# The embedding's rows split early, kept in HBM and fetched by transposing transfers

## The chip, the cores and the metric

The kernel runs on one core of a Trainium2 chip. The time is the device time of one execution in microseconds. Lower is better.

## What is computed

One layer of a hybrid decoder over 2048 prompt tokens and 32 sample tokens (8 sequences of 4), model width 1024: a gated linear attention branch and a causal convolution branch side by side, merged, projected and added to x; then a gate with an embedding that is an input of its own for every token (256 wide). The change touches the last lines of it:

```python
x = x + merged @ w_o
x = x + jax.nn.sigmoid(x @ w_pg) * (p @ w_pe)      # p: (tokens, 256), w_pe: (256, 1024)
y = rmsnorm(x, g_final)
```

## The kernel before, in words

Matrix products are made in f16 with split operands: each f32 operand becomes a high half and a low half (`hl`, L669: one ScalarE operation for the high half, one VectorE operation for the low half), and a product is three matmuls (high by high, high by low, low by high). TensorE contracts over the partitions, so an activation has to stand with its channels on the partitions before it can be an operand.

The last stage (from L664, in the tile pool `p4`) works on pairs of token tiles, 2 x 128 tokens, eight pairs, in two passes:

- The first pass (loop at L846) loads x for the pair from the input, multiplies the merged branches by w_o in a seven-product scheme (`split_forms`, `halves`, L691 to L711, 84 matmuls of 512 columns a pair), adds the results to x in place (`Residual`, L777) and stores x in `x1_d` in HBM (L851). After the first pair the 14 forms of w_pg are loaded and split, two steps a pair.
- The second pass (loop at L866) loads x from `x1_d` (L868), transposes it on TensorE (`transposed`, L839), makes its forms and multiplies them by w_pg in the same scheme. `Gate` (L791) takes each quarter of the result as it comes: `gate` (L750) makes `p @ w_pe` for it (three matmuls for each of two chunks of the embedding, L274 to L276), then tanh, product and sum, and `finish` (L761) makes the norm and stores y.

The embedding comes in through `load_p` (L738): the tile `pr` (128 tokens x 256, f32) is loaded over SP's queue, TensorE transposes it in two pieces (L746) into a PSUM tile, and `hl` (L747) writes the halves `pT`. `Gate.__init__` calls it twice a pair; the 32 sample rows get one call of their own. `pr`, `pT` and the f16 forms have 2, 2 and 10 buffers; x has 4, two pairs' worth.

Loads go over SP's queue (`dma`), stores and accumulating loads over POOL's (`store`). The order on each engine and queue is set by a planner ahead of time from program order and estimated times, and the engines then run in that order: an instruction that waits holds up all behind it on its engine.

Of the kernel before, what the change touches and what calls it, by code (L numbers as in the profile page):

```python
# [9 lines left out]
F32 = mybir.dt.float32  # L10
F16 = mybir.dt.float16
# [8 lines left out]
P = 128  # L20
D = 1024
T = 2048
# [12 lines left out]
PLE = 256  # L35
# [6 lines left out]
SX = 2.0 ** 3  # L42
# [44 lines left out]
def hybrid_step(ctx: ExitStack, tc, A, O):  # L87
    nc = tc.nc
# [8 lines left out]
    dram = ctx.enter_context(tc.tile_pool(name="dram", bufs=1, space=bass.MemoryType.DRAM))  # L97
# [6 lines left out]
    def dma(out, in_):  # L104
        return nc.sync.dma_start(out=out, in_=in_)

    def store(out, in_):
        return nc.gpsimd.dma_start(out=out, in_=in_)
# [7 lines left out]
    def sm_tile():  # L116
        return smp.tile([P, 512], F32, tag="sm", name="sm")
# [101 lines left out]
    def load_w(src, c0, width=P, k0=0, nk=KC, pool=None):  # L219

        c0 = [c0] if isinstance(c0, int) else c0
        w = (pool or wpool).tile([P, 2, nk, len(c0) * width], F16, tag="w", name="w")
        st = wst.tile([P, nk, len(c0) * width], F32, tag="st", name="st")
        for i, c in enumerate(c0):
            wdma(st[:, :, i * width:(i + 1) * width], src[k0 * P:(k0 + nk) * P, c:c + width].rearrange("(k p) c -> p k c", p=P))
        split_w(w[:, 0], w[:, 1], st)
        return w
# [104 lines left out]
    with sb_pool("pg", 2) as pg, sb_pool("p0", 2) as p0:  # L332
# [16 lines left out]
        for gi, nt in enumerate(P0_GROUPS):  # L349
# [9 lines left out]
            r = xt[0][1]  # L359
# [257 lines left out]
    for blk, (a, n, aT, bT, _) in enumerate(ops):  # L617
# [4 lines left out]
        for c in range(KC):  # L622
            m = []
            for i, (w, act, d) in enumerate(((wA[c], aT, ta_d), (wB[c], bT, tb_d))):
                t = p3.tile([P, DB], F32, tag=f"t{i}", name=f"t{i}", bufs=T_BUFS[i])[:, 0:n]
# [27 lines left out]


    x1_d = dram.tile([P, TT // P + 1, D], F32, name="x1_d")
    pp = A["p_prompt"][0, 0]
    psm = A["p_sample"][0].rearrange("b t d -> (b t) d")
    yp = O["y_prompt"][0]
# [5 lines left out]
    with sb_pool("p4", 2) as p4:  # L664
# [4 lines left out]
        def hl(dst, src, sc):  # L669
            S.activation(dst[:, 0], src, AF.Copy, scale=sc)  # L670
            V.scalar_tensor_tensor(out=dst[:, 1], in0=src, scalar=sc, in1=dst[:, 0], op0=MULT, op1=SUB)

        def split_forms(t, sc):

            a11, a12, a21, a22 = (t[:, 4 * k:4 * k + 4, i * P:(i + 1) * P] for i in range(2) for k in range(2))
            sums = [p4.tile([P, 4, P], F32, tag="sum", name="sum", bufs=3) for i in range(3)]
            F = {f: p4.tile([P, 2, 4, P], F16, tag="f", name="f", bufs=10) for f in (A11, A12, S2, S1, S3, A22, S4)}
            hl(F[A11], a11, sc)
            hl(F[A12], a12, sc)
            V.tensor_tensor(out=sums[0], in0=a21, in1=a22, op=SUB)  # L680
            V.tensor_tensor(out=sums[1], in0=sums[0], in1=a11, op=SUB)
            hl(F[S2], sums[1], sc)
            hl(F[S1], sums[0], sc)
            V.tensor_tensor(out=sums[2], in0=a11, in1=a21, op=SUB)
            hl(F[S3], sums[2], sc)
            V.tensor_tensor(out=sums[1], in0=a12, in1=sums[1], op=ADD)
            hl(F[S4], sums[1], sc)
            hl(F[A22], a22, sc)
            return F

        def halves(F, W, got, cut=False):  # L691

            def prod(ps, fa, fb, start, cols=((0, 512),)):
                for c0, w in cols:
                    for k in range(4):
                        for p in range(3):
                            PE.matmul(ps[:, c0:c0 + w], lhsT=F[fa][:, p == 2, k], rhs=W[fb][k // 2][:, p == 1, k % 2, c0:c0 + w],  # L697
                                      start=start and k + p == 0, stop=k == 3 and p == 2, skip_group_check=not start)
            X, Z, Y = mm_tile(), fl_tile(), fl_tile()
            prod(X, A11, B11, True)  # L700
            r1 = got.keep(X, 1)
            prod(Z, A12, B21, True)
            got(0, 0, r1, 1, Z)
            prod(X, S2, T2, False)
            r2 = got.keep(X, 2)
            prod(Y, S1, T1, True)
            y1 = got.part22(Y)
            prod(X, S3, T3, False)
            prod(Y, S4, B22, False)
            got.rest22(y1, X)  # L710
            got(0, 1, r2, -1, Y)  # L711
            prod(X, A22, T4, False, ((0, 256), (256, 256)) if cut else ((0, 512),))
            got(1, 0, None, 0, X)
# [8 lines left out]
        def dec_parts(t, sc):  # L722
            dT = p4.tile([P, 2, 12, TD], F16, tag="dT", name="dT", bufs=1)
            hl(dT[:, :, 0:4], t[:, 0:4], sc)
            hl(dT[:, :, 4:8], t[:, 0:4], -sc)
            hl(dT[:, :, 8:12], t[:, 4:8], sc)
            return dT

        def dec_rows(j, dT, W):
            ps = mm_tile()  # L730
            rows_halves(ps, j, dT, W)
            t = p4.tile([P, 512], F32, tag="tg", name="part", bufs=2)
            S.copy(t, ps)
            ps = fl_tile()
            PE.matmul(ps[0:TD], lhsT=sel[:, 0:TD], rhs=t, start=True, stop=True)
            return ps[0:TD]

        def load_p(i, r):  # L738

            pr = p4.tile([P, PLE], F32, tag="pr", name="pr")  # L740
            dma(pr[0:r], pp[i * P:i * P + r] if i < 16 else psm)
            pT = p4.tile([P, 2, 2, P], F16, tag="pT", name="pT")
            pt = sm_tile()
            pv = pt.rearrange("p (k t) -> p k t", t=P)[:, 0:2, 0:r]
            for k in range(2):
                PE.transpose(pv[:, k], pr[0:r, k * P:(k + 1) * P], ident[0:r, 0:r])  # L746
            hl(pT[:, :, :, 0:r], pv, SX)  # L747
            return pT
# [42 lines left out]
        class Gate:  # L791
            def __init__(self, x, a, last):
                self.x, self.last, self.a = x, last, a
                self.pT = [load_p(a // P + i, P) for i in range(2)]
                self.ss = [p4.tile([P, 4], F32, tag=f"ss{i}", name="ss") for i in range(2)]
                self.n = [0, 0]
# [26 lines left out]
        def x_tile(src, r=P):  # L823
            if r == P:
                x = [p4.tile([P, D], F32, tag="x", name="x", bufs=4) for _ in range(2)]
            else:
                x = [p4.tile([r, D], F32, tag="xd", name="xd", bufs=1)]
            for i, t in enumerate(x):
                dma(t, src(i))
            return x  # L830
# [15 lines left out]
        for pair in range(npair):  # L846
            a = pair * 2 * P
            x = x_tile(lambda i: xf[a + i * P:a + (i + 1) * P])
            halves(split_forms(mT[pair], sc), w_o, Residual(x))
            for i in range(2):  # L850
                store(x1_d[:, 2 * pair + i], x[i])  # L851
            if pair == dec_at:
                x = x_tile(lambda i: xs, TD)
                dT = dec_parts(mT[npair], sc)
                res = Residual(x)
                for j in range(2):
                    res.add(0, j, 1, dec_rows(j, dT, w_o))
                store(x1_d[0:TD, 2 * npair], x[0])
            if pair == 0:
                w_pe = [load_w(A["w_pe"][0], 0, D, k, 1, pool=pool) for k, pool in enumerate((wpool, wpool2))]  # L860
                halves8 = (t[:, i] for _ in range(7) for t in [mpool.tile([P, 2, 2, 2, 512], F16, tag="m", name="wf")] for i in range(2))
                steps = load_forms(A["w_pg"][0], halves8, True)
                w_pg = next(steps)
            for _ in range(2):
                next(steps, None)
        for pair in range(npair):  # L866
            last = pair == npair - 1
            x = x_tile(lambda i: x1_d[:, 2 * pair + i])  # L868
            halves(split_forms(transposed(x, P), SE), w_pg, Gate(x, pair * 2 * P, last), last)
            if pair == dec_at:  # L870
                x = x_tile(lambda i: x1_d[0:TD, 2 * npair], TD)
                pT = load_p(16, TD)
                dT = dec_parts(transposed(x, TD)[:, :, 0:TD], SE)
                ss = p4.tile([P, 4], F32, tag="ss0", name="ss")[0:TD]
                for j in range(2):
                    gate(x[0], ss, j, TD, pT, dec_rows(j, dT, w_pg), j * 512, 512)
                finish(x[0], ss, 2, TD, ysm)
# [265 lines left out]
```

## Time and profile before

| | |
|---|---|
| time, median of 3 runs | 2420.59 us (2420.32 to 2424.48) |
| the profiled execution | 2422.98 us |
| its span, first to last instruction | 2421.2 us |
| TensorE busy | 2326.5 us (96%) |
| VectorE, ScalarE, GpSimd busy | 1678.6, 858.5, 439.5 us |
| last stage, first pass | about 2040 to 2197 us |
| last stage, second pass | about 2197 to 2406 us, then 15 us of finishing |

The profile is one execution. "Busy" counts an engine's running instructions; matmuls overlap, so that a matmul's duration is longer than the time that it adds, and the time from start to start is the one to add up. PE is TensorE, PEld its weight loads, DVE VectorE, ACT ScalarE, POOL GpSimd, SP SyncE, which here only issues transfers. L746 is line 746 of the kernel.

### The profile page before, as it was taken

Reading aid. Unit: us, or ns where it says so; the run is one execution under the profiler, and the core shown is the slowest. Engines: PE = TensorE matmul, PEld = TensorE weight load, DVE = VectorE, ACT = ScalarE, POOL = GpSimd, SP = SyncE. Lnnn points to the kernel's source line nnn. Section 1 sums busy time; section 2 is a strip of 40 time slices with the busy share of each in tenths; the row PEclk is TensorE's granted clock in tenths of the full one; section 3 lists DMA queues with packets and bytes.
Section 4 is the critical chain, followed back from the end, with each engine's and each line's share of the span. In section 5 each row is a group of like instructions: output and inputs, shape, how many; then the busy total and the mean of one; then the engine's idle time right before and its main releaser. Section 6 shows DMA issues by size and latency. Waiting matters only on the chain.

```text
span 2421.2 us, 43469 instructions
## 1 busy us (share of the span) xinstructions
PE 2326.5 (96%) x16909; PEld 1462.8 (60%) x16909; DVE 1678.6 (69%) x3835; ACT 858.5 (35%) x2043; POOL 439.5 (18%) x965
## 2 busy tenths in 40 slices
PE   5899999999999999999999989999999999999997
PEld 3445555655556655555655556556999997444544
DVE  6666996595784875783973965645577788865666
ACT  6552123223223224223233224444233434323544
POOL 1011212221222122222131222121000000111333
PEclk8999999999999999999999999999999999999999
DMA  7322202103221113220123220236345536743222
GB/s 221 111 95 71 59 19 72 34 28 112 66 58 31 35 51 96 62 69 22 31 69 93 55 82 30 82 98 186 100 116 131 130 100 183 202 125 102 90 81 74
DMA packets 193350, 210.04 MB, mean 87 GB/s; under 512 B 39419, under 2 KB 164665, under 8 KB 191608
## 3 DMA queue, kind: packets, MB, share of 16 engines
q1 hardware_dynamic: 169032, 132.28, 20.8%
q0 software_dynamic: 24112, 74.99, 8.9%
q8 instruction: 132, 2.16, 0.4%
q14 instruction: 74, 0.61, 0.1%
HBM read 138.33 MB, written 69.72 MB: 86 GB/s over the span
## 4 chain that ended last, share of the span: by engine, by line
PE 76%; DMA 7%; DVE 6%; issue 4%; POOL 4%; ACT 2%; SPq 0%; DVEq 0%; POOLq 0%; ACTq 0%
PE mm L274 13%; PE mm L275 13%; PE mm L276 13%; PE fl L274 7%; PE fl L275 7%; PE fl L276 7%; PE mm L697 5%; PE fl L697 4%; DMA stf<-in_w_in 2%; POOL ms L196 1%; PE sm L1048 1%; DVE acc L516 1%; PE sm L1049 1%; PE sm L1050 1%; DMA st<-in_w_pg 1%
## 5 line engine op out<-in xcount | busy, mean ns | idle before, releaser
L274 PE MATMUL mm<-xT,w 128*128 128x416 f16 (+2 forms) x1216 | 363.2, 304 | 3.3 <-DVE zz L947 1.7
L275 PE MATMUL mm<-xT,w 128*128 128x416 f16 (+2 forms) x1216 | 363.4, 304 | 0.0
L276 PE MATMUL mm<-xT,w 128*128 128x416 f16 (+2 forms) x1216 | 362.9, 304 | 0.0
L274 PE MATMUL fl<-xT,wf 128*128 128x416 f16 x960 | 329.7, 344 | 12.5 <-DVE ob L327 11.8
L275 PE MATMUL fl<-xT,wf 128*128 128x416 f16 x960 | 329.5, 343 | 0.0
L276 PE MATMUL fl<-xT,wf 128*128 128x416 f16 x960 | 329.1, 343 | 0.0
L516 DVE SCALAR_TENSOR_TENSOR acc<-ue,kvec,acc 128x1024 f32<-128x1024 f32 (+1 forms) x232 | 290.0, 1272 | 0.0
L275 PEld LDWEIGHTS <-w 128*128 128x128 f16 x2496 | 243.2, 98 | 68.3 <-issue 10.3
L274 PEld LDWEIGHTS <-w 128*128 128x128 f16 x2496 | 243.2, 98 | 59.4 <-issue 2.3
L276 PEld LDWEIGHTS <-w 128*128 128x128 f16 x2496 | 243.2, 98 | 57.3 <-issue 2.2
L697 PEld LDWEIGHTS <-f 128*128 128x128 f16 x1356 | 132.5, 98 | 159.4 <-issue 6.2
L275 PE MATMUL mm<-w,xT 128*128 128x512 f16 x512 | 195.1, 381 | 0.0
L276 PE MATMUL mm<-w,xT 128*128 128x512 f16 x512 | 195.1, 381 | 0.0
L274 PE MATMUL mm<-w,xT 128*128 128x512 f16 x512 | 194.9, 381 | 0.0
L697 PE MATMUL mm<-wf,f 128*128 128x512 f16 (+1 forms) x780 | 180.6, 379 | 5.8 <-ACT f L670 3.7
L274 PE MATMUL fl<-bT,w 128*128 128x208 f16 x640 | 161.7, 253 | 0.6 <-ACT ob L325 0.6
L274 PE MATMUL mm<-aT,w 128*128 128x208 f16 x640 | 161.3, 253 | 0.5 <-DMA aT<-a_d 0.5
L275 PE MATMUL fl<-bT,w 128*128 128x208 f16 x640 | 161.7, 253 | 0.0
L276 PE MATMUL fl<-bT,w 128*128 128x208 f16 x640 | 161.7, 253 | 0.0
L276 PE MATMUL mm<-aT,w 128*128 128x208 f16 x640 | 161.5, 253 | 0.0
L275 PE MATMUL mm<-aT,w 128*128 128x208 f16 x640 | 161.5, 253 | 0.0
L516 DVE SCALAR_TENSOR_TENSOR acc<-acc,ksum 128x1024 f32<-128x1024 f32 x120 | 152.5, 1270 | 0.0
(281 smaller groups left out, 4030.8 us busy)
## 6 DMA issues: line engine op xcount, KB each, us to landing
x<-in_x_prompt SPq DMA_DIRECT2D x32, 512.0 KB, 8.0
st<-in_w_in SPq DMA_DIRECT2D x24, 512.0 KB, 10.2
stf<-in_w_in SPq DMA_DIRECT2D x42, 256.0 KB, 6.7
zz_d<-ob POOLq DMA_DIRECT2D x40, 208.0 KB, 2.4
ta_d<-ob POOLq DMA_DIRECT2D x40, 208.0 KB, 2.3
tb_d<-ob POOLq DMA_DIRECT2D x40, 208.0 KB, 2.6
cv<-cv_d SPq DMA_DIRECT2D x80, 104.0 KB, 2.0
zz<-zz_d SPq DMA_DIRECT2D x80, 104.0 KB, 2.1
```

What stands on the lines that cost most here:

```text
L196: E.tensor_scalar(out=x, in0=x, scalar1=scale, scalar2=EPS, op0=MULT, op1=ADD)
L274: PE.matmul(out, lhsT=lh, rhs=rh, start=(k == 0), stop=False)
L275: PE.matmul(out, lhsT=lh, rhs=rl, start=False, stop=False)
L276: PE.matmul(out, lhsT=ll, rhs=rh, start=False, stop=(k == nk - 1))
L516: V.scalar_tensor_tensor(out=out[:, 0:n], in0=src[:, j:j + n], scalar=w1[:, j:j + 1], in1=out[:, 0:n], op0=MULT, op1=ADD)
L697: PE.matmul(ps[:, c0:c0 + w], lhsT=F[fa][:, p == 2, k], rhs=W[fb][k // 2][:, p == 1, k % 2, c0:c0 + w], start=start and k + p == 0, stop=k ...
L1048: PE.matmul(po[:, c], lhsT=qe[:, cc], rhs=st_prev, start=True, stop=False)
L1049: PE.matmul(po[:, c], lhsT=att[:, c], rhs=v[:, c], start=first, stop=True)
L1050: PE.matmul(pu[:, c * DV:(c + 1) * DV], lhsT=kdT[:, cc], rhs=v[:, c], start=True, stop=True)
```

## The change

`split_p`, new, is called in the first pass for each of the pair's two token tiles, right behind the store of x: it loads the tile's embedding rows, splits them as they are (tokens on the partitions) and stores both halves in a new HBM tensor `p_d` of f16. `load_p` no longer loads, transposes and splits for prompt tiles: it issues two transposing transfers on SP's queue, one for each half, that bring the 128 x 256 block of `p_d` into `pT` with the channels on the partitions. For the sample rows all stays as it was. `ph`, the tile that `split_p` fills, takes its two buffers from the same tag as `pT`.

```diff
+    p_d = dram.tile([T, 2, PLE], F16, name="p_d")
...
+        def split_p(i):
+
+            pr = p4.tile([P, PLE], F32, tag="pr", name="pr")
+            dma(pr, pp[i * P:(i + 1) * P])
+            ph = p4.tile([P, 2, 2, P], F16, tag="pT", name="ph").rearrange("p h k t -> p h (k t)")
+            hl(ph, pr, SX)
+            store(p_d[i * P:(i + 1) * P], ph)
+
         def load_p(i, r):
 
+            pT = p4.tile([P, 2, 2, P], F16, tag="pT", name="pT", bufs=2)
+            if r == P:
+                for h in range(2):
+                    nc.sync.dma_start_transpose(out=pT[:, h], in_=p_d[i * P:(i + 1) * P, h])
+                return pT
             pr = p4.tile([P, PLE], F32, tag="pr", name="pr")
-            dma(pr[0:r], pp[i * P:i * P + r] if i < 16 else psm)
-            pT = p4.tile([P, 2, 2, P], F16, tag="pT", name="pT")
+            dma(pr[0:r], psm)
...
             for i in range(2):
                 store(x1_d[:, 2 * pair + i], x[i])
+                split_p(2 * pair + i)
```

## Rows read from the trace of the kernel before

**Rows 1.** The page: busy time and share; TensorE's granted clock in 40 slices

```profile
PE 2326.5 (96%) x16909; PEld 1462.8 (60%) x16909; DVE 1678.6 (69%) x3835; ACT 858.5 (35%) x2043; POOL 439.5 (18%) x965
...
PEclk8999999999999999999999999999999999999999
```

**Rows 2.** Busy time by stretches: the two passes, then three pairs

```profile
core 0: us, PE busy (x) PEld busy (x) DVE busy (x) ACT busy (x) POOL busy (x), PEclk, DMA share, GB/s
2040.00:2196.80 156.80, 154.63 (x750) 68.81 (x749) 110.50 (x167) 50.11 (x76) 18.65 (x24) 0.98 0.58 172
2196.80:2406.30 209.50, 209.50 (x1092) 104.14 (x1091) 136.77 (x224) 102.69 (x225) 70.12 (x136) 1.00 0.25 83
2225.15:2250.64 25.49, 25.49 (x130) 12.87 (x129) 17.34 (x29) 12.70 (x28) 9.99 (x19) 1.00 0.28 93
2250.64:2276.14 25.50, 25.50 (x131) 12.90 (x129) 17.30 (x29) 12.70 (x28) 9.97 (x19) 1.00 0.28 93
```

**Rows 3.** The chain that ended last, over one pair: start, us, what

```profile
2225.15 0.44 PE sm L746 x4
2225.59 2.59 PE fl L697 x12
...
2238.32 0.22 PE sm L276
2238.54 2.59 PE mm L697 x12
2241.13 2.59 PE fl L697 x12
2243.72 0.44 PE sm L839 x4
...
2250.64 0.44 PE sm L746 x4
2251.08 2.59 PE fl L697 x12
2253.67 0.22 PE sm L274
```

**Rows 4.** Groups by shape, 2196 us to the end: busy us, mean ns

```profile
L671 DVE SCALAR_TENSOR_TENSOR pT<-sm,pT 128x256 f16<-128x256 f32 x16 | 6.3, 410 | 0.0
L670 ACT ACTIVATE pT<-sm 128x256 f16<-128x256 f32 x16 | 5.6, 386 | 0.4 <-PE sm L746 0.4
...
L746 PE MATMUL sm<-ident,pr 128*128 128x128 f32 x32 | 5.3, 273 | 0.0
```

**Rows 5.** Busy time by stretches of 20 us, first pass, columns as in rows 2

```profile
2040.00:2060.00 20.00, 18.69 (x77) 7.80 (x76) 17.74 (x31) 8.06 (x14) 1.26 (x1) 0.87 0.79 249
2060.00:2080.00 20.00, 19.83 (x93) 8.91 (x92) 17.75 (x28) 8.72 (x14) 3.59 (x4) 1.00 0.73 190
2080.00:2100.00 20.00, 20.00 (x94) 9.11 (x93) 16.36 (x25) 7.53 (x12) 2.33 (x3) 1.00 0.67 193
2100.00:2120.00 20.00, 20.00 (x95) 9.05 (x93) 16.64 (x25) 6.66 (x10) 4.16 (x5) 1.00 0.81 227
```

**Rows 6.** Waits in the first pass: us in total, times, longest us

```profile
DVE wf L237 <- ACT wf L236: 10.9, 7, 3.1
...
PE mm L697 <- DVE x L777: 1.2, 3, 0.7
```

**Rows 7.** Waits of SP's queue in the first pass, same columns

```profile
SPq L105 <- DMA x_d<-x: 118.0, 15, 16.1
```

**Rows 8.** Instructions on the tensor x_d: duration in ns, min/median/max

```profile
L108 POOL DMA_DIRECT2D x_d<-x x16: 531/558/1045, 2067.1 to 2198.0; - x16
```

**Rows 9.** Timeline of SP's queue: start, us, transfers issued

```profile
2040.56 3.02 SPq L105 DMA_DIRECT2D x<-in_x_prompt  x4
...
2044.27 1.81 SPq L105 DMA_DIRECT2D pr<-in_p_prompt  x2
...
2225.40 0.80 SPq L105 DMA_DIRECT2D pr<-in_p_prompt  x2
2237.08 2.03 SPq L105 DMA_DIRECT2D x<-x_d  x2
```

**Rows 10.** Issue to landing: the tile pr; x loads at 2237 us (last column)

```profile
DMA to landing us min/median/max: 1.9/2.1/11.8
...
x<-x_d SPq DMA_DIRECT2D x2, 512.0 KB, 4.1
```

**Rows 11.** Timeline of TensorE ahead of the first pass: idle time before it, releaser

```profile
2038.73 1.03 PE L697 MATMUL mm<-wf,f 128*128 128x512 f16 x2 [3.67 <-ACT f L670]
```

## The prediction

> **What bounds the kernel now.** I read the page first: TensorE is busy 96% of the span, no other engine over 69%, and its granted clock is over 0.9 of full speed (2.4 GHz) from the second slice on [rows 1]. A busy share is an average, so next the table by stretches, cut at the two passes of the last stage [rows 2]. The second pass (2196.8 to 2406.3 us) has TensorE busy for all of its 209.50 us at full clock, and one pair of token tiles recurs every 25.49 us with 25.49 us of TensorE. In the first pass (2040.0 to 2196.8) TensorE has 154.63 of 156.80 us, and most of the missing 2.2 us lies in the first 20 us. So in both passes the end moves only if TensorE gets less to do, or if something makes it wait. Next the chain of waits over one pair [rows 3]: it stays on TensorE without a break, so its pieces are the issue slots, and their sum is the period. Last the groups by shape, the 20 us stretches of the first pass, the waits and SyncE's queue (SP), for what would be late if something slipped [rows 4 to 11].
>
> **What is removed.** The 32 f32 transposes of the embedding leave the second pass, four a pair. The chain gives them 0.44 us per four [rows 3]; eight pairs make 8 x 0.44 = 3.5 us. It is the slot that counts, not the 273 ns duration of one [rows 4], since durations overlap: 84 products and 24 embedding matmuls at 0.216 us (12 take 2.59), 16 transposes of x and 4 of the embedding at 0.109 us sum to 18.14 + 5.18 + 1.74 + 0.44 = 25.5 us, the period. Since TensorE has no idle time there, the whole 3.5 us comes off, and what is late next is TensorE still: a pair should take 25.05 us. The two transposes of the sample rows stay. Sixteen pairs of a split's two operations (ScalarE 386 ns, VectorE 410 ns each [rows 4]) leave the pass as well; both engines have over 8 us of room in each period [rows 2], so that is worth nothing.
>
> **What is moved to the first pass.** The splits: 16 x 0.386 = 6.2 us of ScalarE and 16 x 0.410 = 6.6 us of VectorE, the price with a PSUM source, taken for the SBUF source too. On average there is room: VectorE is busy 110.5 of 156.8 us, ScalarE 50.1 [rows 2]. But in the first 40 us VectorE is busy 17.7 of 20 us [rows 5], and its update of x (L777) must read a PSUM bank before TensorE may accumulate into it again. The engines run in order, so a split that waits for its rows holds up that update, the other splits and the forms behind it. The trace prices such a wait: VectorE stood 10.9 us, in 7 waits, for the high half of a w_pg form, and TensorE waited for x only 1.2 us in 3 [rows 6], so about 0.11 us for each us lost on VectorE. With 6.6 us of work and about as much waiting the loss is 13 x 0.11 = 1.4 us. Bounds: 0 if all of it falls into VectorE's gaps; 10 us if each of the 6.6 us of work delays a PSUM read directly and the first pair of loads is waited for as well. I take 1 us, nearer to the row, since that was measured with the same kind of wait.
>
> **The transfers of the first pass.** Sixteen loads of 128 KB move to it and sixteen stores of 128 KB are new (128 rows x 512 f16), 4.2 MB. The pass moves 172 GB/s at a DMA share of 0.58 [rows 2], so 297 GB/s when full, and 4.2 MB are 14 us of full DMA: share 0.67 if spread out, 0.93 if all of it falls in the first 80 us, where the share is 0.67 to 0.81 [rows 5]. Two embedding loads already stood there, queued behind four x tiles, and took 11.8 us to land [rows 9, 10]. On SP the loads come between x loads that wait up to 16.1 us for an earlier store of x [rows 7], and the split behind waits with them. On POOL the stores cost 16 x 0.56 = 9 us of issue at the price of a store of x [rows 8], on an engine that is busy 18.65 of 156.8 us; behind a store that waits for its split stand the stores of x (which free buffers for x loads) and the accumulating w_pg loads. All of this is inside the 0 to 10 us above.
>
> **What is added to the second pass.** Thirty-two transposing transfers of 64 KB on SP, four a pair. No such transfer is in this trace. They need a free pT buffer, which the pair before releases with its last embedding matmul (2238.54), and are wanted at 2253.67 [rows 3], so 15.1 us cover four of them. The nearest rows are the plain 128 KB loads of the same rows: 0.40 us to issue and 2.1 us to land in the median, 11.8 us at worst [rows 9, 10]. With four at 0.40 us and 2.1 us they are there by 2242.3; even at 11.8 us for the last it is 2251.9. I take nothing. The upper end is open: if each of the four ran alone and took more than 3.8 us, TensorE would wait.
>
> The traced row has TensorE's transpose at a 0.109 us slot. The Trainium skill's page "VectorE: DVE Perf Modes", in the rules for kernel authors, speaks against this change: transpose 128x128 on TensorE if PSUM will do as the target, and through the DMA crossbar otherwise. Its section on the three transpose paths gives 1309 ns for a crossbar transpose of 128x128; by that, eight such tiles a pair in a row would be an estimated 10.5 us. That is under the 15.1 us, so the sum would be the same by the page; no run here shows it yet.
>
> **The sum.** The profiled execution took 2422.98 us around a span of 2421.2. It becomes 2422.98 - 3.5 + 1.0 = 2420.5. That execution is 2.4 us above the median of the timed ones, 2420.59, so I lower the median by the same 2.5 us: 2418. Only a difference over 0.2%, 4.8 us, can be told from no change by timing this kernel; the forecast is inside that.
>
> **Rivals.**
> 1. *The transposing transfers stand ahead of the x loads on SP.* Two x loads per pair are released by a store, here at 2237.08 [rows 9], and the pT buffers at 2238.54 by TensorE: the planner's order on SP hangs on 1.5 us. If the four transfers come first, x goes 1.5 us later plus four issues of 0.40 to 1.0 us [rows 9], so at 2240.1 to 2242.5; with 4.1 us to land [rows 10] it is there at 2244.2 to 2246.6, wanted at 2243.72 [rows 3]. TensorE then waits 0.5 to 2.9 us in each of the six pairs whose x is loaded like that: 3 to 17 us, say 1.3 x 6 = 8 us. Time: 2418 + 8 = 2426, slower than before. It decides from 4.8 + 2.5 = 7.3 us of waiting, 1.2 us a pair. For it: the 2.5 us in which x is ready ahead of use are thin. Against it: x comes earlier in the program and is released first.
> 2. *The splits hurt the first pass.* Loads late in a stretch with full DMA queues, ScalarE and VectorE waiting in order. Priced at 8 us, in the upper half of its bounds: 2420.6 - 3.5 + 8 = 2425. For it: the 11.8 us and VectorE's 17.7 of 20 us. Against it: DVE's 10.9 us of waits cost TensorE almost nothing.
> 3. *A transpose costs TensorE its duration.* 32 x 0.273 = 8.7 us off: 2420.6 - 8.7 = 2412. Against it: the slots of 0.109 us sum to the period. The Trainium skill's page "TensorE: Matmul & The Clock Gate", section on the PE-mode transpose, gives about 275 ns for one in a kernel, which is the duration of the row; taken as a price it would give this case.
> 4. *The change doesn't do what it says*: the transfers don't fit under the 15.1 us. With 5.2 us for each of four in a row, 20.8 us, TensorE waits 5.7 us in seven pairs: 2418 + 40 = 2458. Waits that long may also lower its clock: after 3.67 us of idle time ahead of the first pass [rows 11] the granted clock was 0.87 over its first 20 us [rows 5].
>
> **How the numbers follow.** Forecast 0.51 (own range 2414.5 to 2422.5), rival 1 0.14, rival 2 0.18, rival 3 0.10, rival 4 0.07. Faster by over 0.2% (under 2415.7): rival 3 and 0.04 of the forecast, 0.14. Slower (over 2425.4): 0.10 of rival 1, 0.09 of rival 2, rival 4, 0.01 of the forecast, 0.27. The rest, 0.59, is within 0.2%. The range takes in forecast, rival 2, half of rival 3 and most of rival 1: 2412 to 2431.
>
> **What would show it.** Right: pairs of the second pass at 25.05 us, TensorE still without idle time there, the first pass still near 156.8 us long. Rival 1 shows as TensorE waiting for x at L839, with SP's four transfers before the x loads; rival 2 as TensorE waiting for x at L777 or a form, behind a split that waits for its load; rival 3 as pairs of 24.4 us; rival 4 as TensorE waiting for pT at L274. The prediction is wrong if the pairs don't shorten by 0.44 us, or if either pass shows TensorE idle for over 5 us.

## The result, and the profile after

| | before | after |
|---|---|---|
| time, median | 2420.45 us (2418.84 to 2424.48) | 2439.23 us (2436.12 to 2443.12) |
| ratio, 95% interval | | 1.0084 [1.0069, 1.0098] |
| the profiled execution, its span | 2422.98, 2421.2 us | 2440.28, 2438.5 us |

The change makes the kernel 18.8 us slower. The prediction had 2418 us and a range up to 2431: wrong in sign and size.

From the page of after, what answers to [rows 1]: TensorE busy, and its granted clock in 40 slices.

```profile
PE 2326.3 (95%) x16877; PEld 1458.6 (60%) x16877; DVE 1681.1 (69%) x3835; ACT 860.9 (35%) x2043; POOL 447.9 (18%) x981
...
PEclk8999999999999999999999999999999999999999
```

These rows hardly show 18.8 us: the same busy time and clock digits, a span 17.3 us longer. (Further down, the page has 17.3 us of idle time ahead of the products at L698, 10.8 of it ended by an update of x, where before has 5.8.) So I cut the last stage at its products, which are the same in every kernel here: the first pass from the start of the first product with w_o to that of the first with w_pg, the second from there to the start of the last; a pair is 84 of them. Busy time of after by passes, which answers to the first two of [rows 2]:

```profile
core 0: us, PE busy (x) PEld busy (x) DVE busy (x) ACT busy (x) POOL busy (x), PEclk, DMA share, GB/s
2034.37:2206.08 171.71, 159.83 (x752) 70.15 (x753) 117.23 (x185) 55.98 (x95) 27.80 (x40) 0.95 0.63 183
2206.08:2425.50 219.42, 210.92 (x1082) 103.05 (x1079) 134.78 (x210) 100.91 (x212) 67.81 (x136) 0.99 0.25 79
```

Cut in the same way, before takes 158.40 and 211.51 us. The first pass is 13.3 us longer and the second 7.9. TensorE stands idle for 11.9 us of the first (2.2 in before) and for 8.5 us of the second (none in before). (The first product starts at 2034.4 in after and at 2038.7 in before; over the profiled kernels that start lies between 2032.2 and 2038.7. So I compare lengths of passes, not ends.)

**The first pass, pair by pair.** The first three pairs of before, then its seventh, columns as above:

```profile
2038.73:2061.43 22.70, 21.23 (x84) 8.67 (x85) 20.41 (x36) 10.35 (x20) 1.26 (x1) 0.86 0.78 243
2061.43:2079.56 18.13, 18.13 (x84) 8.22 (x84) 15.89 (x25) 6.85 (x11) 3.59 (x4) 1.00 0.76 197
2079.56:2097.69 18.13, 18.13 (x85) 8.23 (x84) 14.49 (x22) 7.23 (x12) 2.33 (x3) 1.00 0.65 186
2158.90:2177.02 18.12, 18.12 (x85) 8.22 (x84) 8.20 (x14) 3.15 (x5) 1.08 (x2) 1.00 0.32 117
```

The first three of after:

```profile
2034.37:2059.05 24.68, 21.41 (x85) 8.63 (x86) 21.36 (x39) 11.43 (x23) 2.78 (x3) 0.86 0.79 239
2059.05:2078.89 19.84, 18.29 (x84) 8.22 (x84) 16.31 (x28) 7.18 (x14) 5.64 (x8) 1.00 0.81 207
2078.89:2106.67 27.78, 21.22 (x85) 8.94 (x84) 19.64 (x32) 10.07 (x18) 6.88 (x12) 0.82 0.74 226
```

They lose 2.0, 1.7 and 9.7 us, the whole 13.3; each of the other five pairs is within 0.3 us of before. Though two splits a pair are written in the program, the planner had moved all 16 into the first 80 us (their stores go out from 2047.9 to 2112.2), where VectorE had least room; in the seventh pair it works 8.20 of 18.12 us. The third pair's 9.7 us are 6.56 us without work and 3.1 us at a lower clock (busy 21.22 instead of 18.13 us; granted clock 0.82). The second pair's loss is a wait of 1.56 us at its end. What TensorE waited for, and the other waits of that pass, after (us in total, times, longest), to be held against [rows 6]:

```profile
POOL p_d L108 <- DVE ph L672: 26.7, 7, 7.5
...
ACT ph L671 <- DMA p_d<-ph: 13.5, 5, 6.6
DVE wf L237 <- ACT wf L236: 12.1, 5, 6.3
...
PE mm L698 <- DVE x L790: 10.8, 5, 6.6
ACT ph L671 <- DMA pr<-in_p_prompt: 10.3, 3, 7.2
...
DVE ph L672 <- ACT ph L671: 6.0, 4, 3.5
```

The longest wait of TensorE follows from four engines' queues, each in order of time: TensorE, VectorE, ScalarE, then the accumulating loads of w_pg on POOL, in before and in after (start us, us, engine, line, what, and in brackets the idle time ahead and what ended it).

```profile
2093.38 8.27 PE L698 MATMUL mm<-wf,f 128*128 128x512 f16 x24 [6.56 <-DVE x L790]
2101.49 5.34 PE L698 MATMUL fl<-wf,f 128*128 128x512 f16 x24
```

```profile
2077.81 0.43 DVE L672 SCALAR_TENSOR_TENSOR ph<-pr,ph 128x256 f16<-128x256 f32 x1 [3.53 <-ACT ph L671]
...
2080.90 1.23 DVE L237 SCALAR_TENSOR_TENSOR wf<-st,wf 128x1024 f16<-128x1024 f32 x1
...
2091.50 1.23 DVE L237 SCALAR_TENSOR_TENSOR wf<-st,wf 128x1024 f16<-128x1024 f32 x1 [6.30 <-ACT wf L236]
2092.64 0.69 DVE L790 SCALAR_TENSOR_TENSOR x<-mm,x 128x512 f32<-128x512 f32 x1
```

```profile
2077.36 0.75 ACT L671 ACTIVATE ph<-pr 128x256 f16<-128x256 f32 x2 [6.56 <-DMA p_d<-ph]
...
2079.81 1.06 ACT L236 ACTIVATE wf<-st 128x1024 f16<-128x1024 f32 x1 [0.66 <-DVE f L672]
...
2090.41 1.06 ACT L236 ACTIVATE wf<-st 128x1024 f16<-128x1024 f32 x1 [6.89 <-DMA st<-in_w_pg]
```

Before:

```profile
2061.70 1.21 POOL L248 DMA_DIRECT2D st<-in_w_pg  x1 [13.91 <-DVE x L777]
...
2069.35 1.19 POOL L248 DMA_DIRECT2D st<-in_w_pg  x1 [1.66 <-DVE wf L237]
...
2080.79 1.18 POOL L248 DMA_DIRECT2D st<-in_w_pg  x1 [3.62 <-DVE wf L237]
```

After:

```profile
2059.64 1.25 POOL L248 DMA_DIRECT2D st<-in_w_pg  x1 [6.63 <-DVE ph L672]
...
2068.68 1.22 POOL L248 DMA_DIRECT2D st<-in_w_pg  x1 [4.31 <-DVE ph L672]
...
2082.42 1.24 POOL L248 DMA_DIRECT2D st<-in_w_pg  x1 [2.00 <-DVE wf L237]
```

These are the second, third and fourth accumulating load of the pass. Counted from the first product they go out 2.3, 3.7 and 6.0 us later than in before. Each needs the plain load under it to have landed or the form from the sum so far to be made, so lateness adds up.

It is tempting to blame POOL, which issues these loads and the new stores of the halves (L108) in one order, since two of the rows name a split (ph) behind 6.63 and 4.31 us of idle time. But the same load has 13.91 us of idle time in before, where no such store exists, put down to an update of x that it doesn't need. A name in brackets can be just the last operation of VectorE ahead of the load. In each case the stores ahead of the load had gone out before what the load needs was there: the plain load under the second landed at 2059.0 (issued on SP at 2055.14, landing 3.9 us later), and VectorE finished the forms ahead of the third and fourth at 2068.2 and 2082.1. Each load starts 0.3 to 0.6 us after that, with POOL free.

So the lateness comes from ScalarE's and VectorE's order. Up to the third load it builds up where VectorE has no gap over 0.2 us (2044 to 2067) and four splits more to make, the first behind ScalarE's wait of 7.2 us for its rows. The third load then lands 3.3 us later than in before, counted from the first product, but ScalarE begins the form made from it 6.1 us later. It stands 6.56 us at a split until 2077.36: the tile `ph` has two buffers, and one is free only when an earlier store of halves has landed. VectorE stands 3.53 us behind it, with an update of x next, and this is the 1.56 us of TensorE in the second pair. The store waited for had gone out right behind the third accumulating load and lands with it, 7.9 us after its issue; two stores with no such load just ahead take 2.2 us. All stores of halves of the pass:

```profile
DMA to landing us min/median/max: 2.2/6.0/7.9
```

The fourth load, issued 6.0 us late, takes 8.0 us to land where it took 6.3, and lands at 2090.4. ScalarE and VectorE stand at the form that needs it, and the update of x that frees TensorE's bank (L790) stands behind it on VectorE. After 6.56 us without work, TensorE's first 24 products take 8.27 us where the next 24 take 5.34, at a granted clock of 0.63 over them: part of them ran at half the clock, 1.2 GHz.

**The second pass.** Three pairs, which answer to the last two of [rows 2]:

```profile
2230.70:2260.01 29.31, 26.35 (x123) 12.58 (x121) 16.63 (x27) 12.41 (x26) 10.05 (x18) 0.94 0.27 81
2260.01:2285.91 25.90, 25.27 (x125) 12.36 (x124) 16.47 (x26) 12.60 (x26) 9.09 (x18) 1.00 0.28 92
2285.91:2312.31 26.40, 25.27 (x125) 12.37 (x124) 16.92 (x27) 12.53 (x26) 9.08 (x18) 1.00 0.28 90
```

Before had 25.49 each. The four transposes are gone, but TensorE now waits at its transposes of the next pair's x (L852): 2.96 us in the first of these pairs, for x itself, and 0.63 and 1.13 us in the next two, for a PSUM bank that the gate's multiply still reads.

```profile
2249.80 1.08 PE L852 MATMUL sm<-ident,x 128*128 128x128 f32 x4 [2.96 <-DMA x<-x_d]
...
2277.21 0.66 PE L852 MATMUL sm<-ident,x 128*128 128x128 f32 x4 [0.63 <-DVE tg L770]
...
2303.61 0.66 PE L852 MATMUL sm<-ident,x 128*128 128x128 f32 x4 [1.13 <-DVE tg L770]
```

SP's queue around the first of them, where [rows 9] had the two x loads of 2237.08 back to back:

```profile
2245.43 0.33 SPq L105 DMA_DIRECT2D x<-x_d  x1
2245.92 3.23 SPq L752 DMA_TRANSPOSE pT<-p_d  x2
2251.02 0.33 SPq L105 DMA_DIRECT2D x<-x_d  x1
```

All transposing transfers of after, by their tensor (ns on SP, min/median/max, and their first and last start):

```profile
L752 SPq DMA_TRANSPOSE pT<-p_d x32: 1168/1231/1872, 2113.2 to 2387.4; - x32
```

Two readings fit these rows. Either the transfers, 1.23 us to issue where an x load takes 0.33, make x late, or x comes when it always came and is asked for earlier. The order on TensorE, counted in products from the start of the pass, speaks for the second: the transposes of the next pair's x begin after 132, 216 and 300 products in after, and after 156, 240 and 324 in before; the embedding's products begin after 96, 180 and 264 instead of 108, 192 and 276. The landings agree: the first x tile lands 43.6 us after the pass's first product in after and 43.9 us in before, but TensorE asks for it at 40.8 us instead of 46.6. The planner, with the f32 transposes of the embedding gone, made a new order.

### The profile page after: what moved, and what is told of

Its sections match the earlier page's. It is cut to its first block, busy times and chain, and to the rows that moved or that the text cites. A ratio compares the mean times of both kernels' runs of the same rounds, so it can differ in the third digit from the quotient of the medians.

```text
span 2438.5 us, 43480 instructions
## 1 busy us (share of the span) xinstructions
PE 2326.3 (95%) x16877; PEld 1458.6 (60%) x16877; DVE 1681.1 (69%) x3835; ACT 860.9 (35%) x2043; POOL 447.9 (18%) x981
## 4 chain that ended last, share of the span: by engine, by line
PE 69%; DVE 8%; DMA 8%; POOL 6%; issue 5%; ACT 3%; SPq 0%; POOLq 0%; DVEq 0%; ACTq 0%
PE mm L274 13%; PE mm L275 13%; PE mm L276 13%; PE fl L275 7%; PE fl L274 7%; PE fl L276 7%; PE mm L698 2%; POOL ms L196 2%; PE fl L698 1%; POOL rsq_t L182 1%; PE sm L1062 1%; PE sm L1063 1%; DVE acc L516 1%; PE sm L1064 1%; PE sm L1000 1%
## 5 line engine op out<-in xcount | busy, mean ns | idle before, releaser
L698 PEld LDWEIGHTS <-f 128*128 128x128 f16 x1356 | 133.7, 99 | 175.6 <-issue 22.1
L698 PE MATMUL mm<-wf,f 128*128 128x512 f16 (+1 forms) x780 | 183.8, 386 | 17.3 <-DVE x L790 10.8
```

## The experiments

The time of before moves by some us between groups of runs, so each kernel has its ratio to the runs of before in its own group. The lengths of the passes are those of the profiled execution.

| | time us | ratio [95%] | first pass | second pass |
|---|---|---|---|---|
| before | 2420.45 | | 158.4 | 211.5 |
| after | 2439.23 | 1.0084 [1.0069, 1.0098] | 171.7 | 219.4 |
| e1_splits_only | 2430.73 | 1.0050 [1.0031, 1.0070] | 170.3 | 211.9 |
| e2_traffic_only | 2434.49 | 1.0062 [1.0041, 1.0084] | 171.5 | 212.0 |
| e3_late_splits | 2435.55 | 1.0072 [1.0044, 1.0100] | 167.8 | 219.8 |
| e4_late_and_after_x | 2436.03 | 1.0063 [1.0041, 1.0085] | 166.3 | 217.8 |
| e5_x_held | 2433.15 | 1.0055 [1.0040, 1.0070] | 170.7 | 212.4 |
| e6_splits_store_sp | 2428.46 | 1.0044 [1.0030, 1.0059] | 166.7 | 211.9 |
| e7_early_x_held | 2422.15 | 1.0008 [0.9999, 1.0018] | 159.7 | 213.9 |
| e8_early | 2429.97 | 1.0038 [1.0026, 1.0050] | 159.0 | 220.8 |
| e9_loads_ahead | 2427.42 | 1.0032 [1.0019, 1.0046] | 163.4 | 212.0 |
| e10_early_both_held | 2421.16 | 1.0007 [0.9993, 1.0021] | 158.9 | 210.4 |
| e12_sixth_pair | 2417.39 | 1.0002 [0.9991, 1.0012] | 159.9 | 210.4 |

The two pass lengths together account for the times to within 2.3 us: 12.3 us over before for e1 (ratio 1.0050, 12.1 us), 9.9 for e8 (1.0038, 9.2), at worst 0.6 us under before for e10 (1.0007, 1.7 us over).

**Which pass.** Before, with `split_p` of the change called in the first pass and nothing reading its result.

```diff
                 store(x1_d[:, 2 * pair + i], x[i])
+                split_p(2 * pair + i)
```

> The kernel before with the change's splits and stores in the first pass added, nothing of them used: the second pass loads, transposes and splits as before. Changed against before, the first pass (first w_o product to last store of x) grew from 156.4 to 169.9 us, and the rest from 223.2 to 231.3 us. Theory 1, the splits themselves cost the first pass its 13.5 us: first pass 165 to 172 us, rest 223 us, time 2427 to 2434. Rival, the first pass was slow only through a planner's order that the transposing transfers brought about: first pass within 3 us of 156.4, time 2417 to 2423.

The first pass took 170.3 us and the second 211.9: the first loss belongs to the splits alone, and the second does not come with them.

**What in the splits.** Only load and store, an f32 copy, without ScalarE and VectorE:

```diff
-            hl(ph, pr, SX)
-            store(p_d[i * P:(i + 1) * P], ph)
+            store(p_d[i * P:(i + 1) * P], pr)
```

> The kernel before with the embedding's rows loaded in the first pass and stored again as they are (f32, the same 128 KB each way as the halves), without ScalarE and VectorE touching them; the second pass as before. Theory 1a, the harm is done by the split's two operations standing in ScalarE's and VectorE's order and waiting for loads and stores: first pass within 3 us of 156.4, time 2416 to 2424. Rival 1b, the 4.2 MB more in a stretch with full DMA queues make the w_pg and x loads late: first pass 163 us or more, time 2427 to 2434.

171.5 us: as long without any work on the two engines, but lost elsewhere. The first two pairs are nearly back (23.3 and 18.1 us), and the third takes 30.6. What waits now is POOL (41.1 us in 12 waits for the loads), in front of the loads of w_pg:

```profile
2072.85 0.54 POOL L108 DMA_DIRECT2D p_d<-pr  x1 [2.51 <-DMA pr<-in_p_prompt]
2073.55 0.54 POOL L108 DMA_DIRECT2D x_d<-x  x1 [0.16 <-issue]
2074.09 1.28 POOL L248 DMA_DIRECT2D st<-in_w_pg  x1
```

Here the stores do hold a load: VectorE had made the form that this one needs by 2065.3. So the work of the splits isn't needed for a loss of this size, and 1a falls; the 163 us or more of 1b came true. But the run doesn't part the traffic from the order on POOL, and its stores wait for other things than those of the change. It suggested the order on POOL, which e6 tests.

**Splits in the second half of the pass.** The change, with four splits in each of pairs five to eight, their loads behind the x loads; then the same with the transposing transfers behind both x loads.

```diff
-            dma(pr, pp[i * P:(i + 1) * P])
+            with tc.issue_after(x_loads[-1].ins):
+                dma(pr, pp[i * P:(i + 1) * P])
...
-                split_p(2 * pair + i)
+            for i in range(4 * (pair - 4), 4 * (pair - 3)) if pair >= 4 else ():
+                split_p(i)
```

> The changed kernel with the splits held back: four tiles each behind the x loads of pairs 4 to 7, where VectorE and the DMA queues have more room. The second pass as changed. Theory 1 with theory 2 (the second pass loses by itself, through transposing transfers of 1.2 us each between the x loads on SP's queue, and through embedding products that hold PSUM banks): first pass 155 to 160 us, the rest still 228 to 233 us, time 2424 to 2430. Rival, the second pass lost only because it began badly: time 2416 to 2421.

The first pass took 167.8 us and not the 155 to 160 that I expected. The first three pairs recover, all but 0.7 us in the first, but the fifth goes from 23.87 to 30.66 us: VectorE and ScalarE wait there for splits whose loads have only just been issued (ScalarE 18.1 us in 5 waits, VectorE 21.3 in 7), ahead of updates of x. The loss moved with the splits and their waits.

> As the run with late splits, and the four transposing transfers of a pair issued behind both x loads of that pair. Theory 2a, the x load behind two transposing transfers is the larger loss (2.96 us of waiting and a clock of 0.91 behind it): 3 to 6 us less than the run with late splits, 2419 to 2426. Rival 2b, the embedding products that hold PSUM banks are the loss: within 2 us of the run with late splits.

The same place of the second pass, with both x loads issued ahead of the transfers:

```profile
2245.00 0.63 PE L856 MATMUL sm<-ident,x 128*128 128x128 f32 x4 [2.71 <-DMA x<-x_d]
```

The pairs are as in e3 (27.53 and 27.58, 25.97 and 25.97, 26.42 and 26.43 us; only the last pair differs, 25.99 and 27.93): the transfers don't make x late. Theory 2a falls.

**The order on TensorE.** The change, with the transposes of the next pair's x held behind the sixth product, which puts them after 156, 240 and 324 products again:

```diff
         def transposed(x, r):
+            with ExitStack() as es:
+                if len(sixth) > npair:
+                    es.enter_context(tc.issue_after(sixth[-1].ins))
```

> The change as it is, with one order put back: in the last stage's second pass the transposes of the next pair's x are held behind the sixth big product of the pair before, so that on TensorE they stand after 156 to 170, 240 to 254 and 324 to 338 of the pass's products as in the kernel before, and not after 132, 216 and 300 as in the change. The transposing transfers stay. Theory 2b (the second pass's stalls come from the new order on TensorE: x is asked for before it has landed, and the embedding's products before their PSUM bank is free): the idle of 2.96 us at the x transposes and most of the five idles of 0.35 to 1.13 us behind the gate's multiply go, the clock stays at full in that pass, and the time is 6 to 10 us under the change's 2439.2: 2429 to 2433, with some 223 us from the last store of x to the end where the change has 231. Rival 2a (the 32 transposing transfers, at 1.2 us of SP's queue each, are what makes x and the embedding late): the idles stay or move, and the time stays at 2436 or more.

The second pass fell from 219.4 to 212.4 us, and pairs without idle time took 25.06 us. 2b holds. One wait was left, 2.6 us behind ScalarE's copies out of PSUM in the second pair; e10 follows it.

**POOL's order alone.** e1 with the 16 stores on SP's queue:

```diff
-            store(p_d[i * P:(i + 1) * P], ph)
+            dma(p_d[i * P:(i + 1) * P], ph)
```

> The splits alone in the first pass (second pass as in the kernel before), with one thing changed against the earlier run of that: the 16 stores of the split embedding go out on SP's queue and not on POOL's. Theory 1c (POOL's in-order queue: a store that waits for its split keeps the accumulating loads of w_pg behind it from being issued, and VectorE, which waits for their sum at its place in order, then frees TensorE's PSUM bank late): the fourth accumulating load is issued about 81 us after 2000 as in the kernel before and not at 86, the idle of 6.73 us goes and with it the stretch at half clock, and the time is 2418 to 2424. Rival 1d (the loads of w_pg are late because of what the splits move or because of the work on VectorE and ScalarE, whoever issues the stores): the idle stays near 6 us and the time at 2429 to 2433; a store that waits on SP may in that case also make loads on SP late, and the time is 2433 or more.

3.6 us less in the first pass, and the idle of 6.7 us is gone, but I had expected 2418 to 2424 and got 2428.5. The fourth accumulating load (2079.16) still goes out 3.8 us later than in before, counted from the first product, where e1 has 5.2, though no store of halves is ahead of it on POOL. So the order on POOL isn't what makes these loads late, as the rows of after show too, and neither 1c nor 1d holds as I had put it. ScalarE's waits for stores of halves (15.8 us in e1) are gone. What waits in order now is ScalarE, for the loads of the splits, and once TensorE behind it. Waits of the pass, as above:

```profile
ACT ph L671 <- DMA pr<-in_p_prompt: 26.8, 11, 6.5
...
PE mm L698 <- DVE x L786: 5.1, 5, 1.6
...
PE fl L698 <- ACT ph L671: 2.1, 1, 2.1
```

**The splits elsewhere.** Splits and stores beside the third stage's products, two to a block, with the hold of e5, and without it:

```diff
+            if blk < len(ops) - 2 and c in (2, 6):
+                split_p(2 * blk + c // 4)
...
-                split_p(2 * pair + i)
```

> The splits and their stores are taken out of the last stage and made beside the third stage's products, two to a block, where no accumulating load stands; the second pass has the transposing transfers, and the transposes of x held at their old place as in the run named e5_x_held. Theories 1c and 2b together: the first pass is as long as before (156 us), the second pass has no stall and lacks the 32 transposes on TensorE (8 x 0.44 us): the kernel before minus 2 to 4 us, 2416 to 2418.5. If the traffic beside the third stage costs there what it cost in the first pass, it is 2425 or more; if the transposing transfers themselves cost the second pass something, it is 2420 to 2428.

> As e7_early_x_held, without the hold: the splits beside the third stage, the second pass as in the change. It shows the second pass's loss by itself. Theory 2b: first pass as before, second pass with the change's idles (some 3 us at the x transposes, some 4 us at the gate's bank, and a clock below full around the first), from the last store of x to the end some 231 us: 2423 to 2429, 6 to 10 us above e7_early_x_held. Rival (the second pass's stalls are an after-effect of the late first pass, in phase or in clock): within 2 us of e7_early_x_held.

The first pass is back (159.7 and 159.0 us), with the same traffic elsewhere. Without the hold the second takes 220.8 us, with it 213.9: its loss is its own and no echo of the first pass. (e8's time, 2430.0, is 1.0 us over the range that I had given.) e7 came out at 1.0008, above the 2416 to 2418.5 that I expected: its second pair takes 29.51 us, with 2.61 us of the wait left in e5 and a lower clock behind it.

**Both old places in the second pass.** e7, with the embedding's products held behind their pair's second product:

```diff
+            with tc.issue_after(marks[A12][-1].ins):
                 mm3(pe[0:r], ...)
```

> e7_early_x_held with one more order put back: the products with the embedding are held behind the second big product of their pair, so that the first of a pair stand after 108, 192 and 276 of the second pass's big products as in the kernel before, and not after 96, 180 and 264. Theory 2c (the 2.6 us that TensorE lost in e7_early_x_held at 2237.9, behind ScalarE's copies out of PSUM, come from the embedding's products being too early: the gate's chain then stands ahead of those copies on ScalarE and VectorE): that idle goes, and the pass takes what it took before less 8 x 0.44 us: 2416 to 2419 where the kernel before has 2419.7. Rival 2d (the transposing transfers themselves, at 1.2 to 1.9 us of SP each, or the transfers of y and x, set that wait): an idle of 2 us or more stays in the second pass and the time is 2421 to 2424.

The three pairs that answer to [rows 2], columns as above:

```profile
2215.66:2242.65 26.99, 25.22 (x127) 12.42 (x125) 16.42 (x27) 12.39 (x27) 10.34 (x18) 1.00 0.29 88
2242.65:2267.70 25.05, 25.05 (x126) 12.40 (x124) 16.71 (x27) 12.32 (x27) 10.16 (x18) 1.00 0.35 95
2267.70:2292.76 25.06, 25.06 (x126) 12.42 (x124) 16.73 (x27) 12.33 (x27) 10.16 (x18) 1.00 0.33 94
```

The wait that is left in the first of them:

```profile
2233.57 2.75 PE L710 MATMUL mm<-wf,f 128*128 128x512 f16 x12 [1.77 <-ACT r L820]
```

25.05 us a pair, with all transposing transfers in place: 0.44 us less than before. One wait of 1.77 us stays, smaller than the 2.61 of e7; 2c is right in part. Its row shows ScalarE's copies behind a gate step, and why only that pair has it is open. The time, 1.0007, can't be told from before.

**Loads ahead of their splits.** e6, with eight buffers for loaded rows and four for halves, in tiles that only the second pass uses:

```diff
-            pr = p4.tile([P, PLE], F32, tag="pr", name="pr")
-            dma(pr, pp[i * P:(i + 1) * P])
+            if i % 8 == 0:
+                prs.append(p4.tile([P, KC, 2 * P], F32, tag="xt", name="pr", bufs=1))
+                for j in range(8):
+                    dma(prs[-1][:, j], pp[(i + j) * P:(i + j + 1) * P])
...
```

> The splits alone in the first pass, with the stores on SP as in e6_splits_store_sp, and now with eight buffers for the loaded tiles (in a tile of 8 KB that only the second pass uses) and four for the halves, so that a split finds its tile landed: the loads go out eight at a time, long before their splits. The 32 instructions of ScalarE and VectorE, the 4.2 MB and their number of transfers are those of e6_splits_store_sp. Theory 1e (what harms the first pass is that an engine that works in order stands at a split and waits for the split's own transfer, ScalarE 26.8 us for loads in e6_splits_store_sp and POOL 26.7 us in the change): ScalarE's waits for the embedding's loads fall under 5 us in all, the accumulating loads of w_pg go out as early after the first product as before, TensorE's idles over 1 us in the first pass go, and the time is 2418 to 2423. Rival 1f (the work of the splits on ScalarE and VectorE, 16 x 0.4 us on each, and the traffic in the busiest 60 us are the cost, waits or none): 2425 to 2430 as in e6_splits_store_sp.

163.4 us: another 3.2 off, with ScalarE's waits for the loads down from 26.8 to 10.6 us. 5.0 us were left, so neither 1e nor 1f as I had put them. The waits for loads didn't fall under the 5 us of 1e, and ScalarE has 7.3 us of new ones for stores of the halves, so how much of the 5.0 us is waiting and how much is the work of the splits stays open.

**The whole change, put right.** All 16 splits late in the first pass, loads ahead as in e9, stores on POOL as in the change, and both holds of e10:

```diff
+            with tc.issue_after(marks[A12][-1].ins):
+                hl(ph, prs[-1][:, i % 8], SX)
...
-                split_p(2 * pair + i)
+                if pair == npair - 2:
+                    for k in range(8):
+                        split_p(8 * i + k)
```

> The whole change within the last stage again, with its places put right: the 16 splits stand in the first pass's seventh pair, behind its second big product, where VectorE has 8.2 us of work in 18.1 us and no load of w_pg is left to issue; their loads land ahead of them (eight buffers, as in e9_loads_ahead), their stores are on POOL as in the change; and in the second pass the transposes of x and the embedding's products are held at their old places as in e10_early_both_held. Theory 3 (the first pass loses where the splits stand in its first three pairs, VectorE having 20.4 of 22.7, 15.9 of 18.1 and 14.5 of 18.1 us of work there already, and where an engine waits in order for a split's transfer): the first pass takes 158 to 160.5 us from first to last product as before (158.4; the change 171.7), the second 210 to 211 (211.5 before), and the time is within 3 us of the kernel before. Rival 1f (16 splits and 4.2 MB cost the pass some 5 us wherever they stand, as was left over in e9_loads_ahead: 163.4 us): 162 us or more for the first pass, and 3 to 6 us over the kernel before. Rival 3a (the splits' stores on POOL ahead of the last stores of x, and the splits in a tile that the second pass's transposes of x need, put the loss at the turn between the passes): the first pair of the second pass, 24.6 us in the other runs, takes 27 us or more.

The hold orders the planner's estimate, not the run: on the chip VectorE's splits stand from 2136.2 to 2160.7, in pairs six and seven and not in the seventh alone. These two pairs, columns as above:

```profile
2134.99:2154.25 19.26, 19.26 (x86) 8.27 (x86) 12.62 (x25) 6.49 (x17) 7.50 (x13) 1.00 0.87 237
2154.25:2172.64 18.39, 18.29 (x86) 8.22 (x84) 13.73 (x24) 6.96 (x13) 4.30 (x8) 1.00 0.48 175
```

The seventh has 5.5 us more of VectorE than before and is 0.3 us longer, the sixth is as long as in after; POOL stands 13.6 us at the stores and harms nobody, since no load of w_pg is behind them. Of the pass's remaining 1.5 us, 1.2 are in its first pair (23.89 us), where no split stands. 1.0002 [0.9991, 1.0012]: the change costs nothing once its places are right, and 1f falls. It doesn't beat before either.

## Why the prediction was wrong

- **What bounds the kernel** was read rightly. The term of -0.44 us a pair is right to the hundredth once nothing waits (25.05 in e10), so slots add up and durations don't; rival 3 falls.
- **The first pass is the step that failed most**: "I take 1 us" stands against 13.3. Its price of 0.11 us of TensorE per us of VectorE's waiting was a mean over [rows 6]. The waiting itself was foreseen: VectorE stands 12.1 us for the forms, 10.9 in before, and 6.0 us at the splits, about the 6.6 that the prediction allowed. But TensorE pays 10.8 us instead of 1.2. The longest wait is 6.3 us instead of 3.1. The rows fit a slack of some us ahead of each update of x, under which a wait is free and above which it costs in full; no run tested this by itself. A price per us doesn't carry over to longer waits.
- The prediction named the mechanism, "a split that waits for its rows holds up that update, the other splits and the forms behind it". It left out that a split also waits for an earlier store to land, since `ph` has two buffers: ScalarE stands 13.5 us for that, beside 10.3 us for rows. Its upper end of 10 us counted VectorE's work and no lateness that adds up along the loads of w_pg, nor the 3.1 us at the lower clock. What it feared behind a waiting store on POOL, priced as issue time (16 x 0.56 = 9 us), was not the cost: POOL stands 26.7 us at those stores, but the three late loads of w_pg were each released later, with POOL free.
- From e1 to before, by steps: stores off POOL 3.6 us, loads ahead 3.2, another place for the splits 3.5 (with the stores back on POOL and the second pass changed), and 1.5 left, mostly in a pair without splits. Since each edit gives the planner a new order, the shares are rough; the sum isn't. That the splits in the first pairs are the cause is shown by e1, e7, e8 and e12; how the loss divides among waits, work and traffic there stays open.
- **The transposing transfers at nothing** was right as it was meant. In all of after TensorE waits for no transfer of pT; four take 4 x 1.23 = 4.9 us of SP and land a median 3.0 us after issue, some 8 us in all, inside the 15.1 us. The Trainium skill's page "VectorE: DVE Perf Modes", section on the three transpose paths, has 1309 ns for a 128x128 crossbar transpose; the prediction's estimate of 10.5 us a pair from it compares with these 8 us. Its rule for kernel authors, to use TensorE if PSUM will do, wasn't what decided.
- **The step that was not there** is the second pass's order on TensorE. The sum took 25.49 us, removed 0.44 and left the rest in place. But the order comes from the planner, which drew the transposes of x 24 products and the embedding's 12 products forward; 7.1 us come back by the hold of x alone (219.4 to 212.4) and 3.5 by the hold of the embedding in the kernels with early splits (213.9 to 210.4). Rival 1 named the symptom (TensorE waiting for x at its transposes) and another cause, which e4 excludes.
- Rival 2 had the sign and the stretch, at 8 us for 13.3. Both of the prediction's own tests for being wrong came true in after: pairs of 25.9 to 29.3 us, and 10.8 us of waiting for x in the first pass.

## What to carry to other kernels

Price a moved step by what stands behind it on each in-order queue, and by how late the longest chain behind it becomes, not by the mean cost of waits that fit into slack. Count what its own buffers wait for as well as its inputs. Before you believe the releaser that a wait names, look at the same instruction in the kernel before. Work that a planner may place goes where you say or where it likes: find the pair in which the engine really has room (8.2 of 18.1 us here, against 20.4 of 22.7) and hold it there, with its inputs already landed. After removing anything from the bound engine, compare the order of what is left on it before believing that the rest stands still.

## What the runs showed of the hardware that I had not expected

A transposing transfer of 64 KB costs SP's queue 1.17 to 1.87 us (median 1.23), where a plain load of x, 512 KB, takes 0.33 us.

A store of 128 KB issued right behind an accumulating load of 512 KB landed 0.4 us after it, 6.2 to 7.9 us after its own issue, where two stores without such a load just ahead took 2.2 us. It isn't POOL's queue alone: in e6, a store on SP's queue that went out 1.1 us behind such a load took 7.5 us.

The steps of the norm's square root on GpSimd (L182 and L183, one number a partition) took from 0.28 to 2.2 us each in before and from 0.28 to 1.7 us in after. Two in a row in after:

```profile
2237.44 0.28 POOL L183 TENSOR_SCALAR rsq_y<-rsq_t,rsq_y 128x1 f32<-128x1 f32 x1
2237.70 1.39 POOL L182 TENSOR_SCALAR rsq_t<-rsq_y,ss 128x1 f32<-128x1 f32 x1
```

The long one, and one of 1.13 us behind it, coincide with VectorE's update of y from two SBUF tiles (1.28 us from 2237.76) and the low halves behind it. The Trainium skill's page "GPSIMD Engine Reference", section on specifications, says that GpSimd's SBUF interfaces are shared with VectorE and contended for by its instructions with two SBUF inputs; the rows agree, and no run here tested it.
